# Contrast adjustment on one core: loads and stores in one written order on SyncE's queue, in place of two queues

## The chip, the core and the metric

The kernel runs on one core of a Trainium2 chip. The metric is the device time of one execution in microseconds (us), as a median of several runs. Beside it there is a profile of one execution: the busy time of each engine, the DMA queues with their packets, and the instructions with what they waited for. The engines are named PE (TensorE), DVE (VectorE), ACT (ScalarE), POOL (GpSimd) and SP (SyncE). "L81" is line 81 of the kernel before.

## The reference

The input is 16 images of 3 channels of 512 x 512 float32 values, 50.33 MB. Each channel image (there are 48) is stretched about its own mean and clipped.

```python
def reference(x, factor):            # x: 16 x 3 x 512 x 512, factor: 1.5
    mean = np.mean(x, axis=(2, 3), keepdims=True)
    return np.clip(mean + factor * (x - mean), 0, 1).astype(np.float32)
```

The mean is needed before the first output value, and every value is read once and written once: 100.66 MB in all.

## The kernel before, in words

The 48 channel images lie one behind the other in memory. The kernel cuts them into rows of 8192 values, so that one image is 32 rows, and into 12 tiles of 128 rows x 8192 values: a tile holds four whole images, one row to a partition, 32 KB in each partition, 4 MiB in all. Six such tiles fit the buffer called `ring`; tile t stands in place t modulo 6, and is worked on in place.

`load` (L68 to L76) issues a transfer from `in_x_dram` into the ring, on SyncE's queue. `store` (L100, L101) issues a transfer of a tile, or of some columns of it, from the ring to `out_dram`, on ACT's queue.

`compute(t)` (L78 to L98) does the work on one tile:

- DVE sums the first 4352 columns of each row (L81), while ACT sums the other 3840 (L84, a copy into `junk` with an accumulated sum).
- Two matmuls with a constant block matrix (L86, L87) add up the 32 rows of each image, multiply by (1 - factor) / pixels, and spread the result over the image's rows. What stands in `bias` is the amount to be added to each value.
- DVE multiplies by the factor and adds this amount (L91), then clips to 0 and 1 (L94), both in place.
- The tile is stored. Tile 0 alone goes in two pieces (L89, `FIRST`): 2048 columns are scaled, clipped and stored, then the other 6144.

The order is written out by hand; the framework adds only the waits that the data needs. First come five load instructions for six tiles: tile 0 in two pieces (2048 and 6144 columns), tile 1, then tiles 2 and 3 in one transfer, and tiles 4 and 5 in one. Then, for each tile in turn, `compute(t)` and, while there are tiles left, `load(t + 6)`:

```python
        for t in range(n_tiles):
            compute(t)
            if t + BUFS < n_tiles:
                load(t + BUFS)
```

An engine takes its instructions in the order in which they were written. So three things follow. On ACT, a store waits for DVE's L94 of its tile, and the next tile's sum (L84) stands behind it. On SyncE, the load of tile t + 6 waits until the store of tile t has left the same place of the ring. And as loads and stores are on different queues, both kinds may be under way at the same time. In the profile, q1 is the queue of the loads (SyncE) and q10 that of the stores (ACT).

Of the kernel before, what the change touches and what calls it, by code (L numbers as in the profile page):

```python
# [1 line left out]

# [4 lines left out]


P = 128  # L10
ROW = 8192
BUFS = 6
SHORT = 2048
FIRST = (SHORT, ROW - SHORT)
SUM = 4352


@with_exitstack
def kernel(
    ctx: ExitStack,  # L20
    tc: tile.TileContext,
    x: bass.AP,
    factor: float,
    out: bass.AP,
):

    nc = tc.nc
    f32 = mybir.dt.float32  # L30
    Alu = mybir.AluOpType
    Act = mybir.ActivationFunctionType

    B, C, H, W = x.shape
    n_img, n_pix = B * C, H * W
    ppi = n_pix // ROW
    per_tile = P // ppi
    n_tiles = n_img // per_tile
    assert ppi * ROW == n_pix and per_tile * n_tiles == n_img

    factor = float(factor)
    wconst = (1.0 - factor) / float(n_pix)

    x_f = x.rearrange("b c h w -> (b c h w)")
    out_f = out.rearrange("b c h w -> (b c h w)")

    def dram(ap, t, c0=0, c1=ROW):
        return bass.AP(tensor=ap.tensor, offset=t * P * ROW + c0, ap=[[ROW, P], [1, c1 - c0]])

    consts = ctx.enter_context(tc.tile_pool(name="consts", bufs=1))  # L50
    xpool = ctx.enter_context(tc.tile_pool(name="xpool", bufs=1))
    small = ctx.enter_context(tc.tile_pool(name="small", bufs=1))
    psum = ctx.enter_context(tc.tile_pool(name="psum", bufs=1, space=bass.MemoryType.PSUM))


    sums = small.tile([P, 2 * n_tiles], f32, name="sums")
    junk = small.tile([P, ROW - SUM], f32, name="junk")
    bias = psum.tile([P, n_tiles], f32, name="bias")

    blockw = consts.tile([P, P], f32, name="blockw")  # L60
    nc.gpsimd.memset(blockw, 0.0)  # L61
    for a in range(0, P, ppi):
        nc.gpsimd.memset(blockw[a : a + ppi, a : a + ppi], wconst)  # L63


    ring = xpool.tile([P, BUFS, ROW], f32, name="ring")

    def load(t, c0=0, c1=ROW, n=1):  # L68

        b = t % BUFS  # L70
        src = bass.AP(
            tensor=x_f.tensor,
            offset=t * P * ROW + c0,
            ap=[[ROW, P], [P * ROW, n], [1, c1 - c0]],
        )
        nc.sync.dma_start(out=ring[:, b : b + n, c0:c1], in_=src)  # L76

    def compute(t):  # L78
        xt = ring[:, t % BUFS, :]
        own = sums[:, 2 * t : 2 * t + 2]  # L80
        nc.vector.tensor_reduce(  # L81
            out=own[:, 0:1], in_=xt[:, 0:SUM], axis=mybir.AxisListType.X, op=Alu.add
        )
        nc.scalar.activation(out=junk, in_=xt[:, SUM:ROW], func=Act.Copy, accum_out=own[:, 1:2])  # L84
        shift = bias[:, t : t + 1]
        nc.tensor.matmul(shift, blockw, own[:, 1:2], start=True, stop=False)  # L86
        nc.tensor.matmul(shift, blockw, own[:, 0:1], start=False, stop=True)  # L87
        c = 0
        for n in FIRST if t == 0 else [ROW]:  # L89
            part = xt[:, c : c + n]  # L90
            nc.vector.tensor_scalar(  # L91
                out=part, in0=part, scalar1=factor, scalar2=shift, op0=Alu.mult, op1=Alu.add
            )
            nc.vector.tensor_scalar(  # L94
                out=part, in0=part, scalar1=0.0, scalar2=1.0, op0=Alu.max, op1=Alu.min
            )
            store(t, c, c + n)
            c += n  # L98

    def store(t, c0, c1):  # L100
        nc.scalar.dma_start(out=dram(out_f, t, c0, c1), in_=ring[:, t % BUFS, c0:c1])  # L101

    with tc.manual_schedule():
        load(0, c1=SHORT)
        load(0, c0=SHORT)
        load(1)
        load(2, n=2)
        load(4, n=2)
        for t in range(n_tiles):
            compute(t)  # L110
            if t + BUFS < n_tiles:
                load(t + BUFS)


# [1 line left out]
_INS = ['x', 'factor']  # L116
_OUTS = [((16, 3, 512, 512), 'float32')]

_NUMBERS = {'factor': 1.5}


# [26 lines left out]
```

## Time and profile before

| | before |
|---|---|
| median of 3 runs | 239.11 us (239.05 to 239.17) |
| span of the profiled execution, first to last instruction | 237.3 us |
| what the median has beyond the span | 1.8 us |
| bytes read and written | 50.33 MB + 50.33 MB |
| mean rate over the span | 424 GB/s |
| busy: DVE / ACT / PE | 163.1 us (69%) / 43.2 us (18%) / 14.1 us (6%) |
| one tile on DVE: L81, L91, L94 | 4.68, 4.49, 4.43 us |
| landing of a 4 MiB load / store after its issue, median | 49.7 / 35.8 us |

The page shows the span in 40 equal slices of 5.93 us; a digit is the busy share of a slice in tenths, 9 being 90% or more, and for the DMA row it is the mean over the sixteen DMA engines of the core. For each queue it gives the packets, the bytes and the time that the packets took, as a share of sixteen engines' span. The chain of waits follows back from the last instruction what released each step. Behind these views stand the trace's own records: each instruction with its start and length, each packet of a queue with start, length and size, and the time at which each transfer was reported as landed. A group such as "L81 DVE TENSOR_REDUCE sums<-ring" is an instruction with its line, its engine, and what it writes from what it reads. The time to landing runs from the issue, so it holds the time that a transfer stood behind others.

### The profile page before, as it was taken

How to read it: one execution, taken by the hardware profiler on the slowest of the kernel's cores; microseconds unless marked ns; L12 is line 12 of the kernel's file. 1: busy time of each engine (PE TensorE's matmuls, PEld its weight loads, DVE VectorE, ACT ScalarE, POOL GpSimd, SP SyncE). 2: the span in 40 equal slices, each digit the busy share in tenths (PEclk: the TensorE clock that was granted, in tenths of full speed). 3: DMA queues.
4: the chain of work that ended last, by engine and by line, in shares of the span. 5: the costliest groups of instructions: out<-in, count | busy, mean ns of one | idle time of the engine just before them, and what ended most of it. 6: DMA issues, size and time to landing. Idle time of an engine off the chain costs nothing.

```text
span 237.3 us, 285 instructions
## 1 busy us (share of the span) xinstructions
PE 14.1 (6%) x48; PEld 12.0 (5%) x48; DVE 163.1 (69%) x38; ACT 43.2 (18%) x25; POOL 0.9 (0%) x9
## 2 busy tenths in 40 slices
PE   0010010001010001010010100100100100010000
PEld 0010010001010001010010100100100100010000
DVE  0079989048989328999989898891892795687000
ACT  2050230041050023050320504101400500500000
POOL 1000000000000000000000000000000000000000
DMA  7999999999999999999999999999999999999996
GB/s 297 410 442 442 421 442 359 456 439 441 442 436 414 403 431 442 442 442 442 436 442 436 414 409 425 442 442 442 442 436 442 436 420 403 425 442 442 442 442 265
DMA packets 3712, 100.66 MB, mean 424 GB/s; under 512 B 384, under 2 KB 384, under 8 KB 384
## 3 DMA queue, kind: packets, MB, share of 16 engines
q1 hardware_dynamic: 1840, 50.33, 49.7%
q10 hardware_dynamic: 1872, 50.33, 49.2%
HBM read 50.33 MB, written 50.33 MB: 424 GB/s over the span
## 4 chain that ended last, share of the span: by engine, by line
DMA 57%; DVE 29%; another core or an unknown queue 3%; PE 1%; SPq 1%; issue 0%; DVEq 0%
DMA ring<-in_x_dram 41%; DMA out_dram<-ring 16%; DVE sums L81 10%; DVE ring L91 9%; DVE ring L94 9%; PE bias L87 1%; SPq L76 1%; DVEq L91 0%
## 5 line engine op out<-in xcount | busy, mean ns | idle before, releaser
L81 DVE TENSOR_REDUCE sums<-ring 128x1 f32<-128x4352 f32 x12 | 56.2, 4683 | 45.7 <-DMA ring<-in_x_dram 45.7
L84 ACT ACTIVATE junk<-ring 128x3840 f32<-128x3840 f32 x12 | 40.8, 3403 | 163.3 <-DMA ring<-in_x_dram 107.5
L91 DVE TENSOR_SCALAR ring<-ring,bias 128x8192 f32<-128x8192 f32 (+2 forms) x13 | 54.1, 4163 | 8.9 <-PE bias L87 7.4
L94 DVE TENSOR_SCALAR ring<-ring 128x8192 f32<-128x8192 f32 (+2 forms) x13 | 53.3, 4099 | 0.4
L86 PE MATMUL bias<-sums,blockw 128*128 128x1 f32 x24 | 7.0, 361 | 190.8 <-ACT junk L84 190.8
L86 PEld LDWEIGHTS bias<-sums,blockw 128*128 128x128 f32 x24 | 6.0, 312 | 191.7 <-ACT junk L84 175.2
L87 PE MATMUL bias<-sums,blockw 128*128 128x1 f32 x24 | 7.0, 363 | 4.3 <-DVE sums L81 3.9
L87 PEld LDWEIGHTS bias<-sums,blockw 128*128 128x128 f32 x24 | 6.0, 311 | 5.3 <-DVE sums L81 5.0
L84 ACT ACTIVATION_READ_ACCUMULATOR junk<-ring 128x1 f32 x12 | 2.2, 186 | 0.0
L84 ACT ACT_TABLE_LOAD x1 | 1.3, 1283 | 0.7 <-PEq L129 0.7
L63 POOL MEMSET blockw<- 32x32 f32 x4 | 0.5, 117 | 0.2
L61 POOL MEMSET blockw<- 128x128 f32 x1 | 0.2, 204 | 0.3 <-POOLq L129 0.3
L129 POOL MEMSET const-bfloat16-1.0<- 128x1 bf16 x1 | 0.1, 111 | 0.0
L129 POOL MEMSET const-uint8-127<- 128x1 uint8 x1 | 0.1, 111 | 0.0
L129 POOL MEMSET const-float32-1.0<- 128x1 f32 x1 | 0.1, 108 | 0.0
L129 POOL MEMSET const-float32-0.0<- 128x1 f32 x1 | 0.1, 103 | 0.2 <-issue 0.2
## 6 DMA issues: line engine op xcount, KB each, us to landing
out_dram<-ring ACTq DMA_DIRECT2D x11, 4096.0 KB, 35.8
ring<-in_x_dram SPq DMA_DIRECT2D x7, 4096.0 KB, 49.7
ring<-in_x_dram SPq DMA_DIRECT2D x2, 8192.0 KB, 66.7
ring<-in_x_dram SPq DMA_DIRECT2D x1, 3072.0 KB, 11.7
out_dram<-ring ACTq DMA_DIRECT2D x1, 3072.0 KB, 28.2
ring<-in_x_dram SPq DMA_DIRECT2D x1, 1024.0 KB, 4.8
out_dram<-ring ACTq DMA_DIRECT2D x1, 1024.0 KB, 17.5
```

What stands on the lines that cost most here:

```text
L61: nc.gpsimd.memset(blockw, 0.0)
L63: nc.gpsimd.memset(blockw[a : a + ppi, a : a + ppi], wconst)
L76: nc.sync.dma_start(out=ring[:, b : b + n, c0:c1], in_=src)
L81: nc.vector.tensor_reduce(out=own[:, 0:1], in_=xt[:, 0:SUM], axis=mybir.AxisListType.X, op=Alu.add)
L84: nc.scalar.activation(out=junk, in_=xt[:, SUM:ROW], func=Act.Copy, accum_out=own[:, 1:2])
L86: nc.tensor.matmul(shift, blockw, own[:, 1:2], start=True, stop=False)
L87: nc.tensor.matmul(shift, blockw, own[:, 0:1], start=False, stop=True)
L91: nc.vector.tensor_scalar(out=part, in0=part, scalar1=factor, scalar2=shift, op0=Alu.mult, op1=Alu.add)
L94: nc.vector.tensor_scalar(out=part, in0=part, scalar1=0.0, scalar2=1.0, op0=Alu.max, op1=Alu.min)
L129: nc = _bacc.Bacc("TRN2", target_bir_lowering=False, num_devices=1)
```

## The change

All stores are issued by SyncE, on the queue of the loads. Tile 0 is no longer finished and stored in two pieces. And the order is no longer load and compute in turn: after the six loads at the start, three tiles are computed and stored, three loaded, three computed and stored, three loaded, and then the last six computed and stored. SyncE's instructions in the built program are, in this order: five load instructions for tiles 0 to 5; stores 0, 1, 2; loads 6, 7, 8; stores 3, 4, 5; loads 9, 10, 11; stores 6 to 11. On ACT only the twelve sums remain, on DVE three instructions for each tile.

```diff
-FIRST = (SHORT, ROW - SHORT)
...
-        for n in FIRST if t == 0 else [ROW]:
+        for n in [ROW]:
...
     def store(t, c0, c1):
-        nc.scalar.dma_start(out=dram(out_f, t, c0, c1), in_=ring[:, t % BUFS, c0:c1])
+        nc.sync.dma_start(out=dram(out_f, t, c0, c1), in_=ring[:, t % BUFS, c0:c1])
 
+    half = BUFS // 2
     with tc.manual_schedule():
         load(0, c1=SHORT)
         load(0, c0=SHORT)
         load(1)
         load(2, n=2)
         load(4, n=2)
-        for t in range(n_tiles):
-            compute(t)
-            if t + BUFS < n_tiles:
-                load(t + BUFS)
+        done = 0
+        loaded = BUFS
+        while done < n_tiles:
+            last = loaded == n_tiles
+            for t in range(done, n_tiles if last else done + half):
+                compute(t)
+                done += 1
+            for t in range(loaded, min(loaded + half, n_tiles)):
+                load(t)
+                loaded += 1
```

A store of tile t still waits for L94 of its tile, now on SyncE; a load of tile t + 6 still waits for the store of tile t. All that stands behind such a wait on SyncE, loads and stores alike, waits with it.

## The prediction

> **What bounds the kernel now.** I read the page's table of slices first, then the queues, and only then the chain of waits, since the chain alone would mislead here.
>
> ```profile
> DMA  7999999999999999999999999999999999999996
> GB/s 297 410 442 442 421 442 359 456 439 441 442 436 414 403 431 442 442 442 442 436 442 436 414 409 425 442 442 442 442 436 442 436 420 403 425 442 442 442 442 265
> ...
> q1 hardware_dynamic: 1840, 50.33, 49.7%
> q10 hardware_dynamic: 1872, 50.33, 49.2%
> HBM read 50.33 MB, written 50.33 MB: 424 GB/s over the span
> ...
> DMA 57%; DVE 29%; another core or an unknown queue 3%; PE 1%; SPq 1%; issue 0%; DVEq 0%
> ```
>
> The DMA row is 9 in every slice but the first and the last. The packets of the two queues took 49.7% + 49.2% = 98.9% of what sixteen DMA engines have in 237.3 us, or 234.7 us. The chain's 29% on DVE are stretches in which one transfer waited for DVE while others kept the DMA engines full, so a faster DVE would buy nothing. The bound is bytes through the DMA engines, from the first packet (1.74 us, by the packet records) to the last (236.05 us).
>
> The bytes do not change. What the change can win is therefore only time in which the DMA engines moved bytes slower than they can. I look for that in three ways: the pace with both directions mixed, the pace with one, and what is left over. For the mixed pace, the tile starts on DVE late in the run, which all wait for a load:
>
> ```profile
> 145.67 4.69 DVE L81 TENSOR_REDUCE sums<-ring 128x1 f32<-128x4352 f32 x1 [0.83 <-DMA ring<-in_x_dram]
> ...
> 165.03 4.69 DVE L81 TENSOR_REDUCE sums<-ring 128x1 f32<-128x4352 f32 x1 [4.99 <-DMA ring<-in_x_dram]
> ...
> 184.40 4.68 DVE L81 TENSOR_REDUCE sums<-ring 128x1 f32<-128x4352 f32 x1 [4.99 <-DMA ring<-in_x_dram]
> ...
> 203.76 4.69 DVE L81 TENSOR_REDUCE sums<-ring 128x1 f32<-128x4352 f32 x1 [4.98 <-DMA ring<-in_x_dram]
> ```
>
> They stand 19.36 to 19.37 us apart, and in each interval one tile came in and one went out: 9.685 us for a 4 MiB transfer. For one direction, the records of when transfers landed: loads alone, tile 0 at 12.86 and tile 1 at 22.57, so 9.71; stores alone, the last four at 207.39, 217.09, 226.78 and 236.44, so 9.68. In the packet records a 32 KB packet takes 1213 ns at the median in both queues, alone or mixed (eight of them: 9.70). So **a steady mix of directions costs nothing here**: in 46 to 204 us the two queues alternate packet by packet at full pace.
>
> Something is left over all the same:
>
> ```profile
> 6.00:22.00 16.00, 1.15 (x4) 1.01 (x4) 8.33 (x4) 3.50 (x2) 0.00 (x0) 1.00 1.02 441
> 22.00:46.00 24.00, 1.18 (x4) 1.00 (x4) 19.08 (x5) 3.50 (x2) 0.00 (x0) 1.00 0.99 412
> 46.00:204.00 158.00, 10.56 (x36) 9.02 (x36) 122.31 (x28) 31.65 (x19) 0.00 (x0) 1.00 1.00 432
> 204.00:236.00 32.00, 1.18 (x4) 1.01 (x4) 13.36 (x3) 3.31 (x2) 0.00 (x0) 1.00 0.99 426
> ```
>
> The last column is GB/s. A packet counts where it starts, so a window is blurred by up to one packet on each engine (0.52 MB, 22 GB/s over 24 us); the 412 is only a hint. The sum over the run is firmer:
>
> ```profile
> 1.64 0.42 SPq L76
> ...
> 218.17 0.34 ACTq L101 DMA_DIRECT2D out_dram<-ring  x1
> ```
>
> Tile 1's load is issued at 1.64 and takes 20.9 us to land, 22.54; the last store is issued at 218.17 and takes 18.3, 236.47. Between lie 22 transfers in 213.93 us, and 22 x 9.685 is 213.07. **0.86 us are lost**. The packet records put them where stores begin: SyncE's 32 KB packets that start in 22 to 30 us are over 1213 ns by 0.27 us in sum (divided by 16), those in 34 to 46 us by 0.53 us, with the worst at 1792 ns; those from 46 us on by less than 0.01 us. The first dent is where tile 0's 8 KB store rows join, the second where its 24 KB rows follow. Both may belong to that split store, or to the joining of writes as such.
>
> **The change part by part.** *Tile 0's store in one piece.* DVE loses two instructions: 1.29 + 3.42 + 1.23 + 3.36 = 9.30 us become 4.49 + 4.43 = 8.92. Tile 0 is finished at about 18.33 + 8.95 = 27.3 instead of 27.6; its store may begin 6.4 us later than the first piece did (20.91). Cover: six loads are queued, DMA work until 22.54 + 4 x 9.7 = 61.3 us. Without that cover it would cost 6.4 us. One semaphore write less is 16 packets of 9 ns, nothing; the eight packet pairs of 309 + 912 ns per engine become eight of 1213, 0.06 us less.
>
> *Stores from ACT to SyncE.* ACT loses 13 issues of 0.34 us and the waits that held its sums behind the previous tile's L94 (55.8 us of its idle time). Nothing comes of it on the end: DVE still has about 14.3 us per tile (116.19 to 130.47) against 19.37 us of DMA per tile in and out. SyncE gains 12 issues of 0.34 us, among waits; all its issues are ahead of need, as the next step shows.
>
> *The order.* SyncE now waits in turn: a store for its L94, a load for the landing of the store three places before. Behind each wait stands everything later in the queue, so each issue must be checked against the time at which the DMA engines run dry. At 9.685 us each, from tile 1's landing at 22.5: loads 2 to 5 end at 61.3; stores 0 to 2 at 71.0, 80.7, 90.4; loads 6 to 8 at 100.0, 109.7, 119.4; stores 3 to 5 at 129.1, 138.8, 148.5; loads 9 to 11 at 158.2, 167.8, 177.5; stores 6 to 11 at 187.2 and so on to 235.6. DVE at 14.3 us a tile finishes tiles 0 to 5 at 27.3, 41.6, 56.3, 70.6, 84.9, 99.2; tiles 6 to 8 at 114.4, 128.7, 143.0; 9 to 11 at 172.5, 186.8, 201.1. Issue against need: store 0, 27.3 against 61.3; load 6, 71.0 (store 0 landed) against 90.4; store 3, 90.4 (behind load 8) against 119.4; store 5, 99.2 against 138.8; load 9, 129.1 against 148.5; load 11, 148.5 against 167.8; store 6, 148.5 against 177.5; store 11, 201.1 against 225.9. **The least margin is 19.3 us**, two transfers that are still queued; an issue to a first packet took 1.0 us at the start (0.74 to 1.74). So no wait empties the queue. What is late next is nothing but the bytes.
>
> *What one queue costs at a change of direction.* There are five: in, out, in, out, in, out. No row has one queue turn round. Lower end: 0, the row of 46 to 204 us, where neighbouring packets of an engine go opposite ways at no cost. Upper end: a queue that empties and fills again, 0.4 us (last packet 236.05 to landing 236.44) plus 1.0 us (issue to first packet), 1.4 each, 7 us in all; between them lie 0.27 (the first dent) and 0.49 (what the first 8 KB packets at the start took over 303 ns, in sum). I take 0: the transfers behind are already queued, and the steady mix is the nearest row in what the engines do. A loss below nothing, that is a pace above 9.68, is excluded by the one-way rows.
>
> *The sum.* Low pace: 22.54 + 22 x 9.685 = 235.61. With loads at their own 9.71 and stores at 9.683: 22.54 + 97.1 + 116.2 = 235.84. From landing to the span's end 0.8 us (237.27 - 236.47), and the median stands 1.84 us over the profiled span (239.11 - 237.27): 238.25 and 238.48. I say **238.4**, 0.3% less. A difference under 0.2%, 0.48 us, is about what a measurement of this kernel cannot tell from none.
>
> Two rules of the Trainium skill bear on it. The trace moves 432 GB/s in either direction and in the mix; DMA: Bandwidth & Descriptors (Where 436 GB/s comes from) puts the port ceiling at 435 GB/s but holds that between HBM and SBUF the memory's share of about 358 binds, and the trace contradicts the latter: by 358 the bytes alone would need 281 us, so the memory's directions are not what there is to save. Against the change speaks HBM Reference (Latency): 2 us for an access under high load; if both turns from stores to loads showed it in full, that would be an estimated 4 us, 242.4, which no row here shows.
>
> **The rivals.** *The dent belongs to the joining of writes (0.28).* Then 0.27 us come back at each of the three turns from loads to stores: 238.4 + 0.81 = 239.2, no change. For it: the first dent starts just as stores join. Against: the second dent comes without a new direction, and no dent is seen when loads leave at 203 us.
>
> *Each turn empties the one queue (0.19).* In the mix, one queue may cover the other; now none does. Price 0.45 us, the refill row, five times: 2.25 us, 240.6, slower by 0.6%; to 245 with the upper end. It turns slower from 0.24 us a turn. Against: four ends of one transfer and starts of the next in the same direction (4.6, 11.9, 21.6, and the last stores) show no gap.
>
> *The written order starves the engines (0.03).* It needs my 19.3 us margin wrong; a round trip of 1.4 us at four waits would be 5.6 us, 244. That the change isn't carried out as said I leave aside: the built program has exactly this order on SyncE.
>
> **The numbers.** Forecast 0.50: 238.0 to 238.6, faster. Rival one: same. The other two: slower, 0.22. The range runs from 238.0 (the low sum less 0.25 for the start's own ramp) to 240.7, past the refill price; what lies above has about 0.1.
>
> **What will tell.** Right: the DMA row stays 9, one queue holds 100.66 MB in about 234 us of packets, the last store lands at 235.6 to 235.9, and the packets at 61, 90, 119, 148 and 177 us are as long as the others. Wrong: long packets or gaps there, or an 8 in the DMA row. If store 0 lands later than 71.5 or load 6 is issued after 90, the order failed, not the turns.

## The result

The changed kernel takes 239.93 us (median of 6 runs, 239.78 to 240.05) against 239.14 us for the kernel before (6 runs, 239.05 to 239.30): ratio 1.0031, 95% interval 1.0020 to 1.0041. It is 0.3% slower; 238.4 and 0.3% faster was the forecast. The span of the profiled execution is 237.7 us, 0.4 more than before, and its time 239.88, so 2.2 us lie beside the span in place of 1.87 (that of the kernel before over all its runs here). The 0.79 us are thus about half inside the span and half beside it.

The page of the changed kernel: the DMA row, GB/s by slice, the queue and the chain of waits.

```profile
DMA  7999999999999999999999999999999999999996
GB/s 276 430 441 441 441 441 441 436 403 397 403 430 425 425 436 441 441 441 441 436 408 430 441 414 436 436 441 441 441 425 430 419 436 430 430 430 441 441 441 265
...
q1 hardware_dynamic: 3568, 100.66, 98.8%
...
DVE 4%; issue 0%
```

The DMA row is 9 in every slice but the first and the last, as before, and all bytes are in one queue. The chain is of no use here: it breaks off after 4% of the span. The GB/s row shows what to look for: a stretch of 441 up to 41 us, a weak stretch from 47 to 65 us (403, 397, 403), and mostly good values after it.

SyncE's issues, merged (start, length, instruction, number), show the written order at work:

```profile
27.36 29.40 SPq L100 DMA_DIRECT2D out_dram<-ring  x3
72.04 19.90 SPq L75 DMA_DIRECT2D ring<-in_x_dram  x3
91.99 7.67 SPq L100 DMA_DIRECT2D out_dram<-ring  x3
130.29 20.00 SPq L75 DMA_DIRECT2D ring<-in_x_dram  x3
150.38 52.30 SPq L100 DMA_DIRECT2D out_dram<-ring  x6
```

They come at the forecast times plus 1 us (load 6 at 72.04 for 71.0, load 9 at 130.29 for 129.1), some 19 us ahead of need. Nothing starves: from 8 to 230 us, what fewer than sixteen packets under way leave unused comes to 0.02 us of the sixteen engines' time. Where the 1 us came in is read from the tiles whose start on DVE waited for a load:

```profile
42.01 4.69 DVE L80 TENSOR_REDUCE sums<-ring 128x1 f32<-128x4352 f32 x1 [0.37 <-DMA ring<-in_x_dram]
101.09 4.69 DVE L80 TENSOR_REDUCE sums<-ring 128x1 f32<-128x4352 f32 x1 [1.78 <-DMA ring<-in_x_dram]
159.37 4.69 DVE L80 TENSOR_REDUCE sums<-ring 128x1 f32<-128x4352 f32 x1 [15.33 <-DMA ring<-in_x_dram]
```

These are tiles 2, 6 and 9. From 42.01 to 101.09 six transfers ran (loads 4 and 5, stores 0 to 2, load 6): 59.08 us, and 6 x 9.685 is 58.11, so 0.97 us were lost. From 101.09 to 159.37 again six, with two turns: 58.28, 0.17 lost. From there to the last landing (236.77) eight in 77.40, nothing lost. The packet records name the place: the last load packets before the first store, at 58 to 60 us, take up to 2105 ns in place of 1213.

In what follows **slow packets** means: the time of packets over their usual length (1213 ns for 32 KB, 912 for 24, 303 for 8), where it is more than some 20 ns, added up and divided by sixteen. For packets of 15 KB, which some runs add, 570 ns is scaled from the 32 KB figure; the shortest one seen took 573. The kernel before has 0.46 us of it in the start's first 8 us and 0.80 at 20 to 46 us. The changed kernel has 0.56 at the start, 0.90 at 54 to 64 us and 0.12 afterwards.

### The profile page after: what moved, and what is told of

Same layout as the page of the kernel before. It is cut to its first block, busy times and chain, and to the rows that moved or that the text cites. A ratio compares the mean times of both kernels' runs of the same rounds, so it can differ in the third digit from the quotient of the medians.

```text
span 237.7 us, 281 instructions
## 1 busy us (share of the span) xinstructions
PE 13.9 (6%) x48; PEld 12.0 (5%) x48; DVE 162.5 (68%) x36; ACT 43.2 (18%) x25; POOL 0.9 (0%) x9
## 5 line engine op out<-in xcount | busy, mean ns | idle before, releaser
L90 DVE TENSOR_SCALAR ring<-ring,bias 128x8192 f32<-128x8192 f32 x12 | 53.9, 4492 | 8.9 <-PE bias L86 6.0
L93 DVE TENSOR_SCALAR ring<-ring 128x8192 f32<-128x8192 f32 x12 | 53.1, 4427 | 0.4
```

The source lines that it names most:

```text
L90: nc.vector.tensor_scalar(out=part, in0=part, scalar1=factor, scalar2=shift, op0=Alu.mult, op1=Alu.add)
L93: nc.vector.tensor_scalar(out=part, in0=part, scalar1=0.0, scalar2=1.0, op0=Alu.max, op1=Alu.min)
```

## The experiments

The ratio is always to the kernel before, run beside it. "Beside" is time minus span, as a median.

| kernel | us | ratio (95%) | beside | slow packets, where |
|---|---|---|---|---|
| changed, five turns | 239.93 | 1.0031 (1.0020 to 1.0041) | 2.2 | 0.90 at 54-64 |
| a_six, three turns | 239.78 | 1.0022 (1.0014 to 1.0031) | 2.2 | 1.00 at 54-64 |
| a_two, seven turns | 240.53 | 1.0055 (1.0034 to 1.0075) | 2.2 | 1.05 at 54-64, 0.99 later |
| a_alt, 13 turns | 241.41 | 1.0090 (1.0073 to 1.0107) | 2.2 | 1.10 at 54-64, 0.34 later |
| a_one, one turn | 239.35 | 1.0004 (0.9995 to 1.0013) | 2.2 | 0.31 at 112-122 |
| a_warm | 241.21 | 1.0072 (1.0047 to 1.0097) | 2.2 | 0.78 at 54-64 |
| a_single | 240.24 | 1.0044 (1.0028 to 1.0061) | 2.2 | 1.06 at 54-64 |
| a_lastact | 239.83 | 1.0028 (1.0018 to 1.0039) | 2.2 | 1.11 at 54-64 |
| b_whole | 240.23 | 1.0043 (1.0028 to 1.0058) | 2.2 | 1.07 at 20-46, 0.28 later |
| b_dvesplit | 241.05 | 1.0079 (1.0066 to 1.0091) | 2.55 | 0.93 at 20-46 |
| a_split | 239.44 | 1.0010 (1.0001 to 1.0019) | 1.77 | 1.09 at 54-64 |
| a_six_split | 239.37 | 1.0006 (0.9998 to 1.0015) | 1.79 | 1.12 at 54-64 |
| a_dvesplit | 240.01 | 1.0036 (1.0024 to 1.0048) | 2.2 | 0.98 at 54-64 |
| a_six_stores | 239.75 | 1.0021 (1.0012 to 1.0029) | 2.2 | 1.01 at 54-64 |
| a_stagger | 240.92 | 1.0078 (1.0065 to 1.0090) | 2.2 | 1.66 at 15-28, 0.02 later |
| a_even | 241.19 | 1.0079 (1.0064 to 1.0093) | 2.2 | 1.64 at 20-28, 0.05 later |
| s_first | 240.93 | 1.0066 (1.0053 to 1.0079) | 1.81 | 1.91 at 0-8, 0.01 at 54-64 |
| s_first_small | 239.58 | 1.0012 (1.0003 to 1.0021) | 1.79 | 0.63 at 0-8, 0.67 at 54-64 |
| b_first | 240.37 | 1.0045 (1.0032 to 1.0058) | 1.88 | 1.85 at 0-8, 0.01 at 20-46 |

The time and the ratio are of many executions, the slow packets of one each. That one was the longest of a_two's (241.54 us) and lay 0.7 us over the median of b_whole's (240.96); of a_warm's it was nearly the shortest (239.87).

**First theory after the result:** the first stores of an execution pay about 0.9 us once, and later turns almost nothing. Rivals: each turn costs; or the paired load that ends at 61 us does.

**a_six** and **a_two**: the number of turns.

```diff
-    half = BUFS // 2
+    half = 6      # a_six: six in, six out, six in, six out; a_two has 2 here
```

> The changed kernel in groups of six (six in, six out, six in, six out): three turns of the queue in place of five. Theory 'the first stores pay once' (the long packets at 58 to 60 us, some 0.9 us, come with the first write of an execution, later turns cost 0.1 us or less): they stay, 239.7 to 239.9 us. Theory 'each turn costs': two turns fewer at 0.2 to 0.3 us each, 239.3 to 239.5. Theory 'the paired load ends badly' (the long packets belong to the two-tile load that ends there): stay as they are, 239.7 to 239.9.

> The changed kernel in groups of two until all is loaded (six in, then two out, two in three times, then six out): seven turns in place of five; a load still waits for a store with one transfer of 9.7 us queued behind it, so no gap. First stores pay once: 240.0 to 240.2 us. Each turn costs 0.2 to 0.3 us: 240.3 to 240.5. Paired load: 239.9 to 240.1. If the waits of the written order starve the engines, the DMA row falls under 9 somewhere in 60 to 130 us.

a_six: 239.78, as the first theory has it, with 1.00 us at the first turn and 0.01 at the two others. a_two: 240.53, with 0.69 us of slow packets also at its third turn, near 100 us, and a ragged end (1.1 us of the sixteen engines' time idle after 234 us, against 0.3 in the changed kernel). So a later turn can cost nearly as much as the first, which the first theory does not allow; the runs scatter (240.01 to 241.54).

**a_warm**: a small store early.

```diff
+    warm = consts.tile([P, 64], f32, name="warm")
+    nc.gpsimd.memset(warm, 0.0)
...
         load(0, c1=SHORT)
+        nc.sync.dma_start(out=dram(out_f, 0, 0, 64), in_=warm)
         load(0, c0=SHORT)
```

> The changed kernel with one 64 KB store of zeros (128 x 64 values, into the first columns of tile 0's output, which the real store overwrites) on SyncE's queue behind the first 1 MB load. First stores pay once: the long packets at 58 to 60 us go, at most 0.3 us is added at the start, 239.0 to 239.3 us. Each turn costs: two more turns, 240.2 to 240.5, and the long packets stay. Paired load: long packets stay, 240.0 to 240.2.

The slow packets at the first turn stayed (0.78 us). (The added store is 32 KB, 128 rows of 256 bytes, and not 64 KB.) An early store of this size does not take the loss to itself. The runs scatter from 239.83 to 242.34, and the profiled one took 239.87, so where the others lose up to 2.5 us isn't known.

**a_single**: no paired loads.

```diff
-        load(2, n=2)
-        load(4, n=2)
+        load(2)
+        load(3)
+        load(4)
+        load(5)
```

> The changed kernel with tiles 2 to 5 loaded by four single loads in place of two paired ones. Paired load theory: the long packets at 58 to 60 us shrink to the 0.1 us of the later turns, 239.0 to 239.2 us. First stores pay once, and each turn costs: unchanged, 239.8 to 240.1.

1.06 us at 54 to 64 us: the paired load is not the cause.

**a_alt**: 13 turns; no wait of the written order empties the queue.

```diff
-        done = 0
-        loaded = BUFS
-        while done < n_tiles:
...
+        for t in range(n_tiles):
+            compute(t)
+            if 1 <= t <= BUFS:
+                load(t + BUFS - 1)
```

> The changed kernel with the middle of the order alternating transfer by transfer: six in, two out, then one in and one out in turn until all is loaded, then the last out; 13 turns in the one queue instead of five, each wait still covered by one queued transfer. Theory 'each turn of the one queue costs' (0.2 us a turn, from 239.8 at three turns to 240.5 at seven): about 241.5 us, long packets at the turns from loads to stores. Theory 'the first turn alone pays' (0.9 us once, later turns 0.1 or less, the rest of the difference outside the span): 240.0 to 240.4 us.

241.41, on the figure for "each turn costs". Tile starts on DVE in a_alt, each behind one store and one load, that is two turns:

```profile
130.45 4.69 DVE L80 TENSOR_REDUCE sums<-ring 128x1 f32<-128x4352 f32 x1 [2.50 <-DMA ring<-in_x_dram]
150.00 4.69 DVE L80 TENSOR_REDUCE sums<-ring 128x1 f32<-128x4352 f32 x1 [5.18 <-DMA ring<-in_x_dram]
169.60 4.69 DVE L80 TENSOR_REDUCE sums<-ring 128x1 f32<-128x4352 f32 x1 [5.22 <-DMA ring<-in_x_dram]
189.43 4.69 DVE L80 TENSOR_REDUCE sums<-ring 128x1 f32<-128x4352 f32 x1 [5.45 <-DMA ring<-in_x_dram]
```

They stand 19.55, 19.60 and 19.83 us apart. The same bytes on two queues took 19.36 to 19.37 in the kernel before. So in one queue a pair of turns costs 0.2 to 0.5 us, which the mix of two queues does not pay.

On the mean over the engines, the slow packets after the first turn come to only 0.34 us. But a tile starts when the last part of its load has landed: the trace reports each landing in sixteen parts, and these drift apart. In a_alt the first and the last part of a transfer are 0.64 us apart at 42 us and 1.79 us at the end of the run; in the changed kernel they are 0.44 and 0.72 us apart. The first part of the last store lands at 236.05 us in both. So in the profiled executions all that a_alt ends later (237.84 for 236.77) is this drift. The packet records don't say on which engine a packet ran, so whether the slow packets fall on the same few engines, and so make the drift, stays open.

**a_one**: a single turn. The stores of tiles 0 to 5 are left out, and those of tiles 6 to 11 are issued twice.

```diff
-            store(t, c, c + n)      # in compute
...
-        done = 0
-        loaded = BUFS
-        while done < n_tiles:
...
+        for t in range(n_tiles):
+            compute(t)
+            if t < BUFS:
+                load(t + BUFS)
+            else:
+                store(t, 0, ROW)
+                store(t - BUFS, 0, ROW)
```

> One turn: all twelve loads, then twelve stores of the same size, all in the one queue with the queue never empty. To have room for that the kernel leaves out the stores of tiles 0 to 5 as such: their places in the ring are loaded over, and their part of the output gets the values of tiles 6 to 11 in their stead. Bytes, sums and passes are the same. Each turn costs 0.2 us: 239.3 to 239.5 us. The first turn alone pays 0.9 us: 239.5 to 239.8, with one group of long packets near 119 us. If instead what was lost at 58 to 60 us belongs to the time since the start or to the paired load and not to the turn, it stays at 58 to 60 us.

239.35 (239.00 to 239.67). Up to the turn at 119 us there are no slow packets behind the start's, so they belong to a turn, or to what comes with it, and not to a time. But this first turn has only 0.31 us of them, a third of what it has in the other kernels: its size isn't fixed, and what makes it smaller here is open. From one turn to 13 the ratio grows by 0.0086, 2.06 us, and 0.8 of that is the larger first turn. From three turns (a_six, 1.00 us at the first) to 13 (a_alt, 1.10) it grows by 0.0068, 1.63 us: **0.16 us a turn on the mean**, though not evenly; from three to five it is 0.0009, within the intervals.

**b_whole**: the other part of the change alone, on two queues.

```diff
-        for n in FIRST if t == 0 else [ROW]:
+        for n in [ROW]:
```

> The kernel before with tile 0 scaled, clipped and stored in one piece; stores still on ACT's queue. If the second group of long packets (0.53 us at 34 to 46 us) belongs to the split store, it goes and the first moves to about 28 us: 238.6 to 238.8 us. If the loss belongs to stores joining loads as such, 0.8 to 0.9 us stay in one group: 239.1 to 239.3 us.

Neither: 240.23, 1.07 us slower than the kernel before beside it. This edit, which I had priced at 0.06 us less, costs by itself at least as much as the whole change (1.0043 against 1.0031, intervals that overlap). The slow packets are 1.07 us in place of 0.80, up to 3020 ns long, with 0.28 more later; the end is ragged (1.3 us idle after 234 us); and 0.3 us come beside the span.

**a_lastact**: does the time beside the span go with ACT's queue?

```diff
+        eng = nc.scalar if t == n_tiles - 1 else nc.sync
-        nc.sync.dma_start(out=dram(out_f, t, c0, c1), in_=ring[:, t % BUFS, c0:c1])
+        eng.dma_start(out=dram(out_f, t, c0, c1), in_=ring[:, t % BUFS, c0:c1])
```

> The changed kernel with one store, that of tile 11, issued by ACT. It asks where 0.35 us beside the span come from: the changed kernel and its variants take 2.2 us more than their span, the kernel before 1.87. If that goes with ACT's queue being unused: 1.87 again, so 239.6 us with the span unchanged. If it goes with the length of SyncE's program (22 transfers here, 11 before): 2.2 again, 239.9 us.

2.2 beside the span, so not with ACT's queue. Nor with SyncE's program: b_whole has 2.2 too, with eleven transfers on SyncE.

**a_split** and **a_six_split**: the one queue, with tile 0 split again.

```diff
+FIRST = (SHORT, ROW - SHORT)
...
-        for n in [ROW]:
+        for n in FIRST if t == 0 else [ROW]:
```

> The changed kernel with tile 0 again scaled, clipped and stored in two pieces (2048 and 6144 columns), both stores on SyncE's queue. Theory 'the whole store of tile 0 is what costs' (undoing the split costs the kernel before 1.07 us; the one queue by itself nothing or a little less than that): 238.8 to 239.1 us, the long packets at 58 to 60 us much smaller, and 1.87 us beside the span in place of 2.2. Theory 'the one queue and its turns cost': 239.8 to 240.1 us, as the changed kernel, with the long packets in place.

> Groups of six in the one queue (three turns), with tile 0's store in two pieces. Whole store costs: 238.6 to 238.9 us, below both kernels. Turns cost, 0.15 to 0.2 us each: 0.3 to 0.4 below the run with five turns and the split. Neither: 239.7 to 239.8, as six without the split.

a_split: 239.44, between the two expectations. The time beside the span falls to 1.77, the slow packets stay (1.09 us). **So the one queue with its order costs 0.1% (0.24 us, interval 0.02 to 0.45)**, and the rest of the 0.3% is the split. a_six_split, 239.37, can't be told from the kernel before and is the nearest that a variant with the whole output came; none came below it. By the Trainium skill's DMA: Bandwidth & Descriptors (Issuing engines are not separate DMA queues), it is the same engines that run the transfers of either queue, and a second issuer saves little but issue time; a_split's 0.1% is in keeping with that.

**b_dvesplit**, **a_dvesplit** and **a_six_stores** (this one in groups of six): one half of the split at a time.

```diff
         for n in FIRST if t == 0 else [ROW]:      # b_dvesplit, a_dvesplit
...
-            store(t, c, c + n)
             c += n
+        store(t, 0, ROW)
```

```diff
-            store(t, c, c + n)                    # a_six_stores: DVE whole
+            if t == 0:
+                store(t, 0, SHORT)
+                store(t, SHORT, ROW)
+            else:
+                store(t, c, c + n)
```

> The kernel before with tile 0 scaled and clipped in two pieces but stored in one. It parts what the two halves of the split do. If the 0.33 us beside the span go with DVE's two more instructions: 1.87 beside the span, and the span as with the whole store, 238.0 or so, so 239.9 us. If they go with the number or the size of the stores: 2.2 beside it, 240.2 us. The long packets at 28 to 36 us stay in both cases, as the store is whole.

> The changed kernel with tile 0 scaled and clipped in two pieces but stored in one. Beside the span so far: 1.77 with both halves of the split in the one queue, 2.2 with neither; in the kernel before, 1.87 with both, 2.18 with neither, 2.55 with DVE's half alone. If the two halves add up in the same way here: 2.55 beside the span, 240.2 to 240.4 us. If DVE's two more instructions are what saves: 1.8 beside it, 239.5 us.

> Groups of six in the one queue, tile 0 scaled and clipped whole but stored in two pieces: the other half of the split. If the halves add up (DVE's +0.37, the stores' -0.75): 1.4 beside the span, which with a span of 237.6 is 239.0 us, a little below the kernel before. If the split saves only as a pair: 2.2 beside the span, 239.8 us. The long packets at 58 to 60 us, about 1 us, stay.

The halves don't add up. In the one queue either half alone leaves 2.2 us beside the span, and both together give 1.8; on two queues DVE's half alone gives 2.55. In a_six_stores the smaller first store did not lessen the slow packets either. What sets the time beside the span isn't found. Nor does an edit have to change it: of 100 runs of the kernel before beside these kernels, 99 have 1.82 to 1.94 us and one has 2.24.

**a_stagger**: second theory, that the turn hurts since all sixteen engines turn at the same moment.

```diff
         load(1)
+        nc.sync.dma_start(out=junk[0:8, :], in_=dram(x_f, 0, 0, ROW - SUM)[0:8, :])
```

> The changed kernel with one more load of 8 partitions x 15 KB behind tile 1's load, into the scratch tile junk, which is overwritten later: it puts half of the sixteen DMA engines about 0.57 us (by 27 GB/s on an engine) behind the other half. Theory 'the turn hurts since all engines turn at the same moment': the long packets at 58 to 60 us shrink to less than half, 239.3 to 239.8 us. If the turn hurts each engine by itself: they stay at 0.9 us, and the late half ends later, 240.2 to 240.5 us.

The slow packets left the turn, but came at 22 us in full size, among loads alone. All sixteen parts of the next transfer are late: the first of them lands at 43.35 us, for 41.55 in the changed kernel. The added load also holds back ACT's first sum, to 26 us, so tile 0 is stored from 39.7 us in place of 27.4; that is still 20 us ahead of need.

**a_even**: the same with 16 partitions, so that no engine falls behind.

```diff
+        nc.sync.dma_start(out=junk[0:16, :], in_=dram(x_f, 0, 0, ROW - SUM)[0:16, :])
```

> As the run with a small load of 8 partitions behind tile 1's load, but with 16 partitions, so that all sixteen DMA engines get one 15 KB packet and none falls behind the others. In that run the long packets came at 22 us (1.3 us in sum, on all engines) and none at the first turn. Theory 'the engines lose their common step once': no slip here, so nothing at 22 us and 0.9 us at 58 to 60 us; 0.57 us of transfer added, 240.4 to 240.6 us. Theory 'the first transfer of another kind pays, whatever it is': long packets at 22 us again, none at 58 to 60 us, 240.8 to 241.3 us.

Still at 22 us, without a slip between engines: the second theory falls. The windows hint at the move (last column GB/s; a packet counts where it starts, which can blur 12 us by 0.52 MB or 44 GB/s, so the packet sums of the table are firmer). The changed kernel:

```profile
22.00:34.00 12.00, 1.18 (x4) 1.00 (x4) 11.21 (x4) 3.50 (x2) 0.00 (x0) 1.00 0.98 423
54.00:66.00 12.00, 0.59 (x2) 0.50 (x2) 11.25 (x3) 3.62 (x3) 0.00 (x0) 1.00 0.99 393
```

and a_even:

```profile
22.00:34.00 12.00, 0.98 (x4) 0.93 (x4) 3.08 (x1) 8.28 (x5) 0.00 (x0) 1.00 1.00 393
54.00:66.00 12.00, 1.15 (x4) 1.00 (x4) 11.21 (x4) 2.31 (x1) 0.00 (x0) 1.00 1.01 437
```

393 stands at 54 to 66 us, around the first turn, in the one, and at 22 to 34 us in the other, whose first turn runs at 437.

**s_first**, **s_first_small** and **b_first**: third theory, that the first disturbance pays once, and could pay within the ramp. The first two are a_split's kernel with a small load more, b_first the kernel before with it.

```diff
         load(0, c1=SHORT)
+        nc.sync.dma_start(out=junk[0:8, 0:3840], in_=dram(x_f, 0, 0, 3840)[0:8, :])   # small: 1024 columns
         load(0, c0=SHORT)
```

> The changed kernel with tile 0's store split (239.44 us, 1.1 us in long packets at 58 to 60 us) and the small load of 8 partitions x 15 KB right behind the first 1 MB load, that is within the start's ramp, where packets are slow anyway. If the loss is paid once, by the first disturbance: none at 58 to 60 us and at most 0.3 us more in the ramp; half the engines end 0.57 us later: 238.7 to 239.0 us. If each disturbance pays, or the first turn does: 239.7 to 240.0 us.

> The same with 8 partitions x 4 KB (0.15 us on half of the engines). Paid once by the first disturbance, however small: 238.4 to 238.7 us, below both kernels. A slip must be of some size to count, or the first turn pays anyway: 239.4 to 239.7 us.

> The kernel before with the small load of 8 partitions x 15 KB behind the first 1 MB load. Paid once by the first disturbance: the long packets at 24 to 44 us (0.8 us) go, half the engines end 0.57 us later, 238.7 to 239.1 us. Else: they stay, 239.4 to 239.8 us.

The windows of the kernel before:

```profile
22.00:34.00 12.00, 1.18 (x4) 1.00 (x4) 11.21 (x4) 3.50 (x2) 0.00 (x0) 1.00 0.99 418
34.00:46.00 12.00, 0.00 (x0) 0.00 (x0) 7.87 (x2) 0.00 (x0) 0.00 (x0) 1.00 0.99 406
```

and of b_first:

```profile
22.00:34.00 12.00, 0.00 (x0) 0.00 (x0) 11.93 (x5) 3.20 (x1) 0.00 (x0) 1.00 1.02 438
34.00:46.00 12.00, 1.17 (x4) 1.00 (x4) 9.84 (x3) 0.30 (x2) 0.00 (x0) 1.00 1.00 431
```

It moves as the third theory has it: with the 15 KB load ahead, no slow packets are left where stores first join (0.01 us), on one queue or two. But the price is not hidden by the ramp: it is 1.4 us there, more than the 0.8 to 1.1 us saved. The 4 KB load does not bring it on; 0.67 us stay at the turn. ACT's table load, at 0.74 us in the kernel before, is later in all of these (13.24 to 15.09 us), in s_first_small too, where the slow packets stay at the turn; so that it is later isn't what moves them.

## Why the prediction was wrong, step by step

**The bound and the order: right.** The DMA engines are full from end to end, no wait of the written order empties the queue, and DVE, ACT and the matmuls stay off the path. The rival that the order starves the engines is out.

**"0.86 us are lost", to be won back: the step that failed first.** The loss was there, and in the right place. But I booked it to the joining of two streams and took it to go with the second queue. It comes when the first store stream starts, or with another odd transfer ahead of it, and the one queue pays it as well: 0.90 us for 0.80. The first rival had named this ("the dent belongs to the joining of writes"), only with 0.27 us at each of three turns in place of 0.9 at the first. The argument that I held against it, that the second dent comes without a new direction, does not decide it: in b_whole, with tile 0's store whole, both dents are one group of 1.07 us at the first store.

**"Tile 0's store in one piece", priced at 0.06 us less: wrong in size and sign.** b_whole shows 1.07 us more on two queues; on one it is 239.93 against 239.44, ratios 1.0031 and 1.0010, so about 0.5 us. Some 0.4 of the latter lies beside the span.

**"The median stands 1.84 us over the span": a constant carried over that isn't one.** It is 2.2 in the changed kernel and moved between 1.77 and 2.55 in the variants, with no transfer moved in some of them.

**"I take 0" for a change of direction in one queue: too low, within the bounds named.** 0.16 us a turn on the mean over ten more turns, scattered, and in a_alt as drift between the parts of a transfer and not as idle engines; in the changed kernel's profiled execution 0.12 us in sum over its four later turns. Turns from loads to stores at 119 us cost 0.08 and at 177 us 0.04; the turn at 91 us cost nothing that shows. The Trainium skill's HBM Reference (Latency) has 2 us for an access under high load, and the estimate made of it, 2 us for a turn from stores to loads, is out: the pairs of turns in a_alt, each with such a turn, cost 0.2 to 0.5 us. The 0.45 us of the second rival, called the refill row, is none of the rows named (0.27, 0.49 and 1.4).

**One of the signs named does not part what it should.** Store 0 landed at 71.98 us, later than 71.5, which was to mean that the order failed. It was issued at 27.36, 34 us ahead of need, and load 6 at 72.04, well before 90; what made it late are the slow packets at 58 to 60 us.

The sum with what the profiled execution shows: 238.4, plus 0.90 for the first turn, 0.12 for the others, 0.36 beside the span and 0.10 for a start that was slower in this execution (0.56 for 0.46): 239.9, as measured.

**What stays open.** What the engines do in the slow packets: stores of tiles and a load of 15 KB rows bring them on, a 32 KB store of 256-byte rows and a load of 4 KB rows do not, and neither paired loads nor a slip between engines are needed for it. Why a_one's first turn pays a third, and a_two's third turn again. And what sets the time beside the span. All are known by size and not by cause.

## What to carry to other kernels

When a sum over the run leaves a remainder, find out whether it recurs before crediting an edit with removing it: here 0.8 us sat where two streams joined, and it came back with the start of the stores in every order tried (0.8 to 1.1 us, in a_one 0.3), unless an added load drew it, for a higher price. A small edit that rides along with the named change has to be measured alone; here un-splitting one store cost 0.5 us on one queue and 1.07 on two, and moving all stores 0.24. And when a profile shows full transfer engines at the same pace in both directions and in the mix, an order of transfers has little to win: here a turn in one queue cost 0.16 us on the mean, and the steady mix on two queues ran at the pace of one direction.

## What the runs showed of the hardware that was not expected

- One queue pays for a change of direction, some 0.16 us on the mean from three turns to 13, with the sixteen parts of a transfer drifting apart (0.64 to 1.79 us in a_alt), while two queues that alternate packet by packet run at 9.685 us for 4 MiB, the pace of either direction alone (9.68 to 9.71).
- About 0.8 to 1.1 us of slow packets (32 KB packets of up to 2 to 3 us in place of 1213 ns) come at the first tile-sized stores of nearly every order tried (a_one: 0.31), and mostly only there (a_two: 0.69 again at its third turn); an odd load of 15 KB rows ahead draws them to itself, even among loads alone.
- The time beside the span isn't a constant of the program's frame: 1.87, 2.18 and 2.55 us in three kernels on two queues (before, b_whole, b_dvesplit) that differ by two DVE instructions and one store.
